# A hybrid decoder step on one core: four weight units split in the value projection and kept in DRAM, key squares in large tiles, norm factors two steps later

## The chip, the cores and the metric

The kernel runs on one core of a Trainium2 chip as one program. The metric is the device time of that program in microseconds; lower is better. The engines of the core are named as in the profile: PE (TensorE, matrix products; PEld is its weight load), DVE (VectorE), ACT (ScalarE), POOL (GpSimd) and SP (SyncE, which here only issues transfers). Sixteen DMA engines move data between DRAM and the on-chip memory (SBUF); PE writes its results into banks of PSUM.

## The reference

Two layers of a decoder trunk in float32, over one prompt of 1024 tokens and eight single tokens with state from before. The first layer mixes tokens by a gated recurrence (RG-LRU), the second by grouped-query attention in a window of 128 with a sink for each head. Behind each mixer stands a squared-ReLU MLP, ahead of each block an RMS norm, and each block is added to the residual. The part that matters here:

```python
def qkv_heads(x, w_qkv, q_g, k_g):
    q, k, v = jnp.split(x @ w_qkv, [Q_DIM, Q_DIM + KV_DIM], axis=-1)
    q = rms_norm(q.reshape(n, t, N_KV, GROUP, HEAD_DIM), q_g)
    k = rms_norm(k.reshape(n, t, N_KV, HEAD_DIM), k_g)
    v = v.reshape(n, t, N_KV, HEAD_DIM)

def swa_prompt(x, w_qkv, q_g, k_g, sinks, w_out, w_buf):
    q, k, v = qkv_heads(x, w_qkv, q_g, k_g)
    ...
    o = sink_attention(qb, with_prev(k), with_prev(v), dist, mask[:, None, None], sinks)
    y = o.reshape(n, t, Q_DIM) @ w_out

def sq_relu_mlp(x, w_up, w_down):
    return jnp.square(jax.nn.relu(x @ w_up)) @ w_down
```

The model width is 1024, the query width 1024 (16 heads of 64), keys and values 256 each, the MLP's inner width 4096.

## The kernel before

**Data.** Activations lie transposed: eight tiles of 128 channels by 1032 tokens (1024 and the 8 single ones), worked on in three chunks of 344 tokens. A weight matrix comes in units of 128 x 1024 elements (512 KB). A float32 value goes to PE as a rounded upper half and the rest, each in PE's own format: three products (upper by upper, lower by upper, upper by lower) replace one. For this each unit is loaded into a "raw" tile, ACT casts the upper half ("wh", L180) and DVE subtracts it from the raw to get the lower ("wl", L181), for units of the attention in two pieces of 128 x 512 each. The list `units` fixes the order of the loads; `ensure(k)` splits all units up to k and has the next two raw tiles fetched; `unit(name, j)` hands a split unit to its product.

**Stages.** 0 to 330 us: the recurrent layer. Then the first MLP to 958 us, whose products (L582) follow a table of steps, `PROG`, built on Strassen's scheme. Then attention to about 1303 us with its output projection, and from about 1318 us the second MLP.

**Attention.** Query tile 0 and key tile 0 are projected first; then the second key tile (`proj_steps`, L912), the values (`v_proj`, L942), and the query tiles 1 to 7 as filler, whose steps stand between the 32 steps g of the scores. At step g the scores (bank "SS", one buffer, L1006) are masked, exponentiated, transposed (bank "T", L1033), copied by ACT (L1035), multiplied by DVE (pt, L1037) and taken to the values on PE (bank "O", one buffer, L1053). The outputs go to DRAM (od) and come back in three chunks (oh, ol; `load_o`, L1179). From g = 22 the filler is the early part of the second output projection ("wo1", L241), in the order 4, 5, 0, 1, 2, 3 of its inputs; inputs 4 and 5 stay on chip, inputs 0 to 3 come back by `load_o`. Its weight units 0 to 3 are split one by one at g = 20, 21, 23 and 24.

**Key norm.** A chunk of keys leaves PSUM by `take_out`: ACT squares it into one small tile (sq, L820) and copies it into another (x, L821). The two key tiles' norms then run one after the other (`k_evac`, `k_norm`): PE adds the squares across channels into bank "N" (one buffer, L827), DVE reads that bank (L828) and so gives it back, then some steps on ACT and DVE make the factor, and the key's halves are sent on by SP and POOL.

**Order.** Each engine runs its rows strictly in the order of the program that a scheduler wrote down from the data and buffer dependences; the score steps are pinned in the order of the code. SP issues transfers in its own order, and the eight semaphores of its queue rotate, so that a transfer also waits for the one eight places ahead to have landed. A tile of a pool (A 33 large, W 12, S 9 small ones, R 2 raw) is handed out again when its last reader is done.

**Norm factors.** In both MLPs the sum of squares of the last chunk is turned into the factors of the norm at step 7 of `PROG` (`factors`, then `swap_small`); the factors are read first at step 12.

Of the kernel before, what the change touches and what calls it, by code (L numbers as in the profile page):

```python
# [10 lines left out]
F32 = mybir.dt.float32  # L11
# [51 lines left out]
def trunk(ctx: ExitStack, tc: tile.TileContext, I, O):  # L63
# [38 lines left out]
    def A(s="a"):  # L102
        return A2(s)[:, 0:T]
# [4 lines left out]
    def S(s="s"):  # L108
        return small["pool"].tile([P, CH], F32, tag="S", name=nm(s))
# [30 lines left out]
    def cs(c):  # L140
        return slice(c * CH, (c + 1) * CH)
# [25 lines left out]
    def fetch(n):  # L167
        while len(raws) < min(n, len(units)):
            name, _, src, _ = units[len(raws)]
            if name[:2] == "dn":  # L170
                raws.append(small["pool"].tile([P, D], F32, tag="Q", name=nm("raw")))
            else:
                raws.append(R("raw"))
            sp.dma_start(raws[-1][:, 0:src.shape[1]], src)
# [9 lines left out]
    units = []  # L184
    loaded = {}

    def add_units(name, src, n, alloc=lambda j: W):
# [23 lines left out]
    def ensure(k):  # L211
        while nloaded[0] <= min(k, len(units) - 1):
            n, j, _, alloc = units[nloaded[0]]
            fetch(nloaded[0] + (NRAW if n[:2] == "dn" else 2))
            if alloc is None:
                loaded[(n, j)] = raws[nloaded[0]]
            else:
                loaded[(n, j)] = split_unit(raws[nloaded[0]], alloc, dve,
                                            2 if nloaded[0] < 4 or n in ("q", "k", "v", "wo1") else 1)
            nloaded[0] += 1  # L220
# [431 lines left out]
    def mlp_products(layer, tok, pw, r, acc, gnext, store):  # L652
# [25 lines left out]
        for n, (kind, q, i) in enumerate(PROG):  # L678
            up = kind == "up"
            w, x = BY[i]  # L680
            if up and n in (1, 3, 5, 7, 9):
                tok.make(("B22", "T3", "T2", "T4", "T1")[n // 2])
            if n == 7:
                factors(rs.pop("late"), DB())
                swap_small(f"u{layer}", 3)
# [116 lines left out]
    def attention(hs):  # L802
# [14 lines left out]

        def take_out(o):
            s, x = S("sq"), S("x")
            act.activation(s, o, AF.Square)  # L820
            act.copy(x, o)  # L821
            return s, x
# [104 lines left out]
        def vblk(b, p):  # L927
            h = b // 4
            o = (b % 4) * 256 + p * P
            return v_tiles[h][:, o:o + P]  # L930

        def v_proj():
            w = [unit("v", 0, 1), unit("v", 1, 1)]

            def mms(o, sl):
                n = 0
                for k in range(M8):
# [3 lines left out]
                    for xt, wt in ((xh, wh), (xh, wl), (xl, wh)):  # L941
                        pe.matmul(o, lhsT=r_(xt[:, sl]), rhs=r_(wt[:, ws]), start=(n == 0), stop=(n == 3 * M8 - 1))  # L942
                        n += 1

            for b2 in range(NB // 2):
                ps = B("S")
                for j in range(2):
# [5 lines left out]
                if b2 == 3:  # L953
                    vo = S("vo")
                    act.activation(vo[:, :256], ps[:, 256:512], AF.Copy, scale=fx["rt"][:, NB - 1:NB])
                    sp.dma_start(O["v"], vo[:, :256])
            ps = B("T")
            mms(ps[:NS, :256], slice(SEQ, T))
# [181 lines left out]
        for rows in ((1, 0, 3, 2), (5, 4), (7, 6)):  # L1140
            for i, c, o in firsts:
# [4 lines left out]
                if rows[-1] == 4 and i:  # L1146
                    tokens(rs["sq"][:, cs(c)], c)
        sk, xk = A("sk"), A("xk")
        for i, c, o in firsts:
            if i:  # L1150
                act.activation(sk[:, cs(c)], o, AF.Square)
                act.copy(xk[:, cs(c)], o)
            else:
                q_evac(0, c, o)

        def keys(c, o):
            sx = take_out(o)
            k_evac(0, c, (sk[:, cs(c)], xk[:, cs(c)]), fx["row"][:, cs(c)])
            if c == 0:
                by_token()  # L1160
            return lambda: k_evac(1, c, sx, fx["row"][:, cs(c)])
# [36 lines left out]

        NG = 4 * NB
        AHEAD, G0 = 2, 22  # L1200
        FILL = {0: 51, 6: 90, 14: 136, G0: 177}
# [37 lines left out]
        for g in range(NG):  # L1239
# [21 lines left out]
            if g == 17:  # L1261
                for t in (4, 5):
                    ohl[t] = (A("oh"), A("ol"))
            if g in (20, 21, 23, 24):
                ensure(index["wo1", (20, 21, 23, 24).index(g)])
            if g == G0 - 1:
# [371 lines left out]
```

## Time and profile before

| | us |
|---|---|
| median of three runs | 1947.93 |
| lowest and highest run | 1946.99 and 1949.74 |
| the profiled execution's own time | 1948.49 |
| its span in the profile | 1946.7 |
| granted TensorE clock | 1.0 |
| busy: DVE, ACT, POOL | 1482.5, 1010.0, 364.4 |

The page cuts the span into 40 equal slices and gives the busy share of each in tenths; this is how the work of the engines lies over the stages:

```
DVE  7996747987777968787753777589877779687884
ACT  6585635443434635555654666465443436455552
POOL 1320000000000322332123667000000003223321
DMA  5111242244445778888744436622443447788877
```

A slice is 48.7 us. The attention lies in slices 20 to 27: there POOL works too, and the DMA engines reach 6 tenths just before the output projection's end. Durations of groups stand behind a bar as the busy time and the mean of one in ns, then the idle time ahead of them with what ended it. In a timeline a row has the start, the duration, the engine and line, and in brackets the wait ahead of it.

### The profile page before, as it was taken

To read this page: it belongs to the slowest core of one execution; us is meant where nothing else is said; L and a number is where in the kernel's file an instruction comes from. 1 tells how busy PE (TensorE), PEld (TensorE's weight loads), DVE (VectorE), ACT (ScalarE), POOL (GpSimd) and SP (SyncE) were. 2 spreads that over 40 slices of the span, in tenths; PEclk is the share of its full clock that TensorE was granted. 3 is DMA by queue.
4 is the path that set the end of the run, shared out by engine and by line. 5 is a ranking of instruction groups with operands and counts; after the bars stand their busy time and mean duration, and the time that the engine had idled before them with its cause. 6 is when DMAs were issued, how large, how long until landed. Compare 5 with 4: busy or idle time off the path is not lost.

```text
span 1946.7 us, 34178 instructions
## 1 busy us (share of the span) xinstructions
PE 1932.7 (99%) x12820; PEld 1797.6 (92%) x12820; DVE 1482.5 (76%) x2713; ACT 1010.0 (52%) x1999; POOL 364.4 (19%) x709
## 2 busy tenths in 40 slices
PE   9999999999999999999999999999999999999999
PEld 9999999999999999999999887999999999999998
DVE  7996747987777968787753777589877779687884
ACT  6585635443434635555654666465443436455552
POOL 1320000000000322332123667000000003223321
PEclk9999999999999999999999999999999999999999
DMA  5111242244445778888744436622443447788877
GB/s 195 35 46 53 77 160 84 99 164 158 141 155 171 264 207 196 213 237 217 203 124 112 111 108 199 209 84 99 163 147 137 162 167 260 216 193 218 235 197 183
DMA packets 114149, 311.34 MB, mean 160 GB/s; under 512 B 17464, under 2 KB 43072, under 8 KB 113984
## 3 DMA queue, kind: packets, MB, share of 16 engines
q0 software_dynamic: 31264, 105.77, 22.5%
q1 hardware_dynamic: 57376, 135.68, 21.0%
q10 hardware_dynamic: 25344, 67.71, 9.7%
q8 instruction: 101, 1.65, 0.4%
q14 instruction: 64, 0.52, 0.1%
HBM read 179.67 MB, written 116.75 MB: 152 GB/s over the span
## 4 chain that ended last, share of the span: by engine, by line
PE 91%; DVE 4%; ACT 3%; DMA 1%; issue 1%; POOL 0%; SPq 0%; DVEq 0%; ACTq 0%
PE bD L582 37%; PE bZ L582 27%; PE bP L241 10%; PE bS L241 6%; PE bT L241 3%; PE bP L912 3%; PE bO L1053 1%; PE bSS L1006 1%; ACT se L1019 1%; PE bS L942 1%; DVE op L432 1%; PE bT L1033 1%; PE bP L1144 0%; DMA raw<-w_in 0%; DVE wl L181 0%
## 5 line engine op out<-in xcount | busy, mean ns | idle before, releaser
L582 PEld LDWEIGHTS bD<-tl,op 128*128 128x128 f32 x3072 | 385.5, 188 | 11.7 <-DVE ho L733 0.6
L582 PE MATMUL bD<-tl,op 128*128 128x260 f32 x3072 | 389.2, 282 | 0.2
L582 PEld LDWEIGHTS bD<-op,op 128*128 128x128 f32 x3072 | 380.4, 188 | 7.8
L582 PE MATMUL bD<-op,op 128*128 128x260 f32 x3072 | 382.9, 282 | 0.0
L595 POOL DMA_DIRECT2D tl<-hsum x224 | 131.5, 662 | 897.8 <-PE bD L582 411.7
L431 ACT CAST op<-ws 128x512 fp32r<-128x512 f32 (+1 forms) x288 | 162.1, 572 | 255.6 <-DVE ws L550 128.2
L582 PE MATMUL bZ<-tl,op 128*128 128x512 f32 x1152 | 288.2, 394 | 0.0
L582 PE MATMUL bZ<-op,op 128*128 128x512 f32 x1152 | 282.1, 394 | 0.0
L582 PEld LDWEIGHTS bZ<-op,op 128*128 128x128 f32 x1152 | 210.5, 188 | 43.8 <-ACT he L718 0.2
L582 PEld LDWEIGHTS bZ<-tl,op 128*128 128x128 f32 x1152 | 207.9, 188 | 40.4 <-DVE tl L439 0.4
L439 DVE TENSOR_TENSOR tl<-tl 128x520 fp32r<-128x520 f32 (+1 forms) x224 | 145.3, 691 | 76.2 <-ACT tl L438 76.2
L431 ACT CAST op<-raw 128x512 fp32r<-128x512 f32 (+1 forms) x216 | 123.5, 573 | 145.8 <-PE bD L582 82.5
L432 DVE TENSOR_TENSOR op<-ws,op 128x512 fp32r<-128x512 f32 (+1 forms) x288 | 176.0, 625 | 8.6 <-ACT op L431 8.4
L432 DVE TENSOR_TENSOR op<-raw,op 128x512 fp32r<-128x512 f32 (+1 forms) x216 | 134.8, 625 | 7.2 <-ACT op L431 6.3
L438 ACT CAST tl<-tl 128x520 fp32r<-128x520 f32 (+1 forms) x224 | 124.9, 626 | 4.6 <-DMA tl<-hsum 1.9
L733 DVE TENSOR_TENSOR ho<-bD,ho 128x520 f32<-128x520 f32 x140 | 97.4, 696 | 37.3 <-PE bD L582 35.3
L181 DVE TENSOR_TENSOR wl<-raw,wh 128x512 fp32r<-128x512 f32 (+1 forms) x72 | 61.0, 868 | 31.4 <-ACT wh L180 14.9
L722 DVE TENSOR_TENSOR ho<-bZ,ho 128x512 f32<-128x512 f32 x72 | 49.5, 688 | 43.7 <-PE bZ L582 43.2
L724 ACT COPY he<-bZ 128x512 f32<-128x512 f32 x68 | 39.9, 587 | 80.5 <-PE bZ L582 66.0
L706 ACT COPY he<-bZ 128x512 f32<-128x512 f32 x72 | 42.0, 583 | 74.7 <-PE bZ L582 73.6
L733 DVE TENSOR_TENSOR he<-bD,he 128x520 f32<-128x520 f32 x70 | 48.8, 696 | 37.5 <-PE bD L582 37.3
L180 ACT CAST wh<-raw 128x512 fp32r<-128x512 f32 (+1 forms) x72 | 53.0, 764 | 43.6 <-PE bT L241 14.2
(372 smaller groups left out, 3653.9 us busy)
## 6 DMA issues: line engine op xcount, KB each, us to landing
tl<-hsum POOLq DMA_DIRECT2D x128, 260.0 KB, 6.4
raw<-w_up SPq DMA_DIRECT2D x64, 512.0 KB, 4.2
tl<-hsum POOLq DMA_DIRECT2D x96, 256.0 KB, 6.5
raw<-w_dn SPq DMA_DIRECT2D x64, 384.0 KB, 6.2
hsum<-ts ACTq DMA_DIRECT2D x32, 520.0 KB, 4.0
hsum<-ho ACTq DMA_DIRECT2D x32, 516.0 KB, 3.6
hsum<-he ACTq DMA_DIRECT2D x32, 516.0 KB, 2.7
spill<-ho POOLq DMA_DIRECT2D x32, 516.0 KB, 6.8
```

The costliest lines, as they stand in the source:

```text
L180: act.copy(r_(hi[:, sl]), raw[:, sl])
L181: eng.tensor_tensor(r_(lo[:, sl]), raw[:, sl], hi[:, sl], ALU.subtract)
L241: pe.matmul(o, lhsT=r_(wt[:, col(k):col(k) + P]), rhs=r_(xt[:, cs(c)]), start=(k == first and a == 0), stop=(k == final and a == 2))
L431: act.copy(r_(hi), x)
L432: dve.tensor_tensor(r_(lo), x, hi, ALU.subtract)
L438: act.copy(r_(hi), lo)
L439: eng.tensor_tensor(r_(lo), lo, hi, ALU.subtract)
L582: pe.matmul(d[:, 512 * b:512 * b + c], lhsT=r_(wt[:, j * P:j * P + P]), rhs=r_(xt[:, c * b:c * b + c]), start=first and j == 0 and a == 0, ...
L595: pool.dma_start(t[:, n:2 * n], src)
L722: dve.tensor_tensor(o0, d, o[:, HP], ALU.add)
L733: last["sum"] = dve.tensor_tensor(t, inner(d), t, ALU.add).ins
L912: pe.matmul(o, lhsT=r_(wt[:, k * P:k * P + P]), rhs=r_(xt[:, cs(c)]), start=(k == 0 and a == 0), stop=(k == M8 - 1 and a == 2))
```

## The change

It has four parts. `split_to_store` is new: in the value projection, for each of the four pairs of blocks, one of the units 0 to 3 of wo1 is loaded into a large tile (pl), cast (ph) and subtracted in place in two pieces, and both halves are stored in DRAM (eight stores of 512 KB). `fetch` leaves those units out, and `ensure` loads the two halves straight into the tiles of the product (eight loads of 512 KB), two units at g = 17 and two at g = 21. The squares and copies of both key tiles are written into two pairs of large tiles (`held`). And `factors` with `swap_small` stands at step 9 of `PROG` instead of step 7, in both MLPs.

```diff
@@ -166,7 +166,10 @@
 
     def fetch(n):
         while len(raws) < min(n, len(units)):
-            name, _, src, _ = units[len(raws)]
+            name, j, src, _ = units[len(raws)]
+            if (name, j) in stored:
+                raws.append(None)
+                continue
             if name[:2] == "dn":
                 raws.append(small["pool"].tile([P, D], F32, tag="Q", name=nm("raw")))
             else:
@@ -183,6 +186,7 @@
 
     units = []
     loaded = {}
+    stored = {}
 
     def add_units(name, src, n, alloc=lambda j: W):
         for j in range(n):
@@ -212,7 +216,11 @@
         while nloaded[0] <= min(k, len(units) - 1):
             n, j, _, alloc = units[nloaded[0]]
             fetch(nloaded[0] + (NRAW if n[:2] == "dn" else 2))
-            if alloc is None:
+            if (n, j) in stored:
+                loaded[(n, j)] = alloc("wh"), alloc("wl")
+                for t, d in zip(loaded[(n, j)], stored[(n, j)]):
+                    sp.dma_start(t[:, 0:D], d)
+            elif alloc is None:
                 loaded[(n, j)] = raws[nloaded[0]]
             else:
                 loaded[(n, j)] = split_unit(raws[nloaded[0]], alloc, dve,
@@ -680,7 +688,7 @@
             w, x = BY[i]
             if up and n in (1, 3, 5, 7, 9):
                 tok.make(("B22", "T3", "T2", "T4", "T1")[n // 2])
-            if n == 7:
+            if n == 9:
                 factors(rs.pop("late"), DB())
                 swap_small(f"u{layer}", 3)
             if (kind, q, i) == ("up", NU, 4):
@@ -815,8 +823,8 @@
         den = [cp.tile([P, 12], F32, name=f"den{i}") for i in range(3)]
         dd = aux[:, 2 * P + 2 * NS:2 * P + 2 * NS + 4]
 
-        def take_out(o):
-            s, x = S("sq"), S("x")
+        def take_out(o, c, sx):
+            s, x = [y[:, cs(c)] for y in sx]
             act.activation(s, o, AF.Square)
             act.copy(x, o)
             return s, x
@@ -929,6 +937,18 @@
             o = (b % 4) * 256 + p * P
             return v_tiles[h][:, o:o + P]
 
+        def split_to_store(n, j):
+            stored[n, j] = [tc.dram_tile([P, D], F32, name=f"{n}{j}{x}") for x in "hl"]
+            lo, hi = A("pl")[:, 0:D], A("ph")[:, 0:D]
+            sp.dma_start(lo, units[index[n, j]][2])
+            yield
+            for x in (slice(0, D // 2), slice(D // 2, D)):
+                act.copy(r_(hi[:, x]), lo[:, x])
+                dve.tensor_tensor(r_(lo[:, x]), lo[:, x], hi[:, x], ALU.subtract)
+            for d, x in zip(stored[n, j], (hi, lo)):
+                sp.dma_start(d, x)
+            yield
+
         def v_proj():
             w = [unit("v", 0, 1), unit("v", 1, 1)]
 
@@ -942,7 +962,11 @@
                         pe.matmul(o, lhsT=r_(xt[:, sl]), rhs=r_(wt[:, ws]), start=(n == 0), stop=(n == 3 * M8 - 1))
                         n += 1
 
+            ready = iter(())
             for b2 in range(NB // 2):
+                next(ready, None)
+                ready = split_to_store("wo1", b2)
+                next(ready)
                 ps = B("S")
                 for j in range(2):
                     b = 2 * b2 + j
@@ -954,6 +978,7 @@
                     vo = S("vo")
                     act.activation(vo[:, :256], ps[:, 256:512], AF.Copy, scale=fx["rt"][:, NB - 1:NB])
                     sp.dma_start(O["v"], vo[:, :256])
+            next(ready, None)
             ps = B("T")
             mms(ps[:NS, :256], slice(SEQ, T))
             vo = S("vo")
@@ -1145,17 +1170,17 @@
                                   start=(k == 1 and a == 0), stop=(k == 6 and a == 2))
                 if rows[-1] == 4 and i:
                     tokens(rs["sq"][:, cs(c)], c)
-        sk, xk = A("sk"), A("xk")
+        held = [(A("sk"), A("xk")) for _ in range(2)]
+        out = []
         for i, c, o in firsts:
             if i:
-                act.activation(sk[:, cs(c)], o, AF.Square)
-                act.copy(xk[:, cs(c)], o)
+                out.append(take_out(o, c, held[0]))
             else:
                 q_evac(0, c, o)
 
         def keys(c, o):
-            sx = take_out(o)
-            k_evac(0, c, (sk[:, cs(c)], xk[:, cs(c)]), fx["row"][:, cs(c)])
+            sx = take_out(o, c, held[1])
+            k_evac(0, c, out[c], fx["row"][:, cs(c)])
             if c == 0:
                 by_token()
             return lambda: k_evac(1, c, sx, fx["row"][:, cs(c)])
@@ -1197,6 +1222,7 @@
         fill = filler()
 
         NG = 4 * NB
+        AT = (17, 17, 21, 21)
         AHEAD, G0 = 2, 22
         FILL = {0: 51, 6: 90, 14: 136, G0: 177}
         EARLY = {G0 + 0.3: 0, NG: 48}
@@ -1261,8 +1287,8 @@
             if g == 17:
                 for t in (4, 5):
                     ohl[t] = (A("oh"), A("ol"))
-            if g in (20, 21, 23, 24):
-                ensure(index["wo1", (20, 21, 23, 24).index(g)])
+            for _ in range(AT.count(g)):
+                ensure(nloaded[0])
             if g == G0 - 1:
                 for t in range(4):
                     load_o(t, cs(0))
```

**What moves: the key-norm sums on PE.** Rows of PE around the sum of the second key tile's second chunk (the bank is bN, its squares sq before and sk in a large tile now; bP is the second key projection's third chunk and bS the value projection). Before, in the value projection:

```order
L942 MATMUL bS1383_10827<-wh1378_10813,hh1290_10267 128x256
L942 MATMUL bS1383_10827<-wl1379_10814,hh1290_10267 128x256
L942 MATMUL bS1383_10827<-wh1378_10813,hl1291_10268 128x256
L827 MATMUL bN1361_10712<-sq1354_10682,con_73 128x344
L942 MATMUL bS1383_10827<-wh1378_10813,hh1287_10251 128x256
L942 MATMUL bS1383_10827<-wl1379_10814,hh1287_10251 128x256
```

Now, in the key projection's third chunk, whose first eight products stand between this sum and the one before it (the sum of the first key tile's chunk, also in bank N):

```order
L920 MATMUL bP1358_10706<-hl1236_9855,wh1329_10555 128x344
L920 MATMUL bP1358_10706<-hh1235_9854,wl1330_10556 128x344
L920 MATMUL bP1358_10706<-hh1277_10150,wh1329_10555 128x344
L920 MATMUL bP1358_10706<-hl1278_10151,wh1329_10555 128x344
L835 MATMUL bN1359_10710<-sk1317_10513,con_73 128x344
L920 MATMUL bP1358_10706<-hh1277_10150,wl1330_10556 128x344
```

The sum stood behind 24 products of the third key chunk and 15 of the values, and now stands behind 8 of the key chunk.

**What moves: ACT at the end of the value projection.** Before (vt and vo are the scaled values and the value output, qc the copy of the first query tile's sums, wh a unit's upper half):

```order
L952 ACTIVATE vt1299_10325<-bS1385_10929,st_330 128x256 x2
L180 CAST wh1391_11068<-raw1380_10819 128x512 x2
L952 ACTIVATE vt1299_10325<-bS1386_10980,st_330 128x256 x2
L955 ACTIVATE vo1387_11031<-bS1386_10980,st_330 128x256
L960 ACTIVATE vo1389_11059<-bT1388_11034,st_330 8x256
L868 COPY qc1395_11085<-bN1394_11084 128x256
L311 ACTIVATE q1399_11112<-qs1397_11109,st_330 128x16
```

Now (ph is the upper half of a w_out unit that goes to DRAM):

```order
L976 ACTIVATE vt1299_10325<-bS1387_10952,st_330 128x256 x2
L183 CAST wh1395_11108<-raw1376_10815 128x512 x2
L976 ACTIVATE vt1299_10325<-bS1390_11014,st_330 128x256 x2
L979 ACTIVATE vo1391_11065<-bS1390_11014,st_330 128x256
L946 CAST ph1386_10950<-pl1385_10949 128x512 x2
L985 ACTIVATE vo1393_11099<-bT1392_11074,st_330 8x256
L946 CAST ph1389_11012<-pl1388_11011 128x512 x2
L876 COPY qc1399_11125<-bN1398_11124 128x256
L319 ACTIVATE q1403_11152<-qs1401_11149,st_330 128x16
```

Four casts of ph, in two rows of two, stand between the value output vo and the copy qc; the last two wait for the load of pl that SP issues behind the value output.

**What moves: DVE and SP ahead of the output projection.** Rows of DVE from the subtraction for wo1's unit 0 to unit 1 before (se is the score tile, lo a query's lower half, st the single tokens' part, den the sums of the exponentials, pt the transposed probabilities):

```order
L181 TENSOR_TENSOR wl1645_12986<-raw1559_12354,wh1644_12985 128x512 x2
L1014 TENSOR_TENSOR se1302_10330<-bSS1646_12991,se1302_10330 128x4x128
L853 TENSOR_TENSOR lo1648_13029<-bP1639_12945,hi1647_13028 128x344
L1015 TENSOR_REDUCE den2_10323<-se1302_10330 128x4
L857 TENSOR_TENSOR st_330<-bP1639_12945,st_330 64x8
L1016 SCALAR_TENSOR_TENSOR den2_10323<-den2_10323,st_330 128x4
L857 TENSOR_TENSOR st_330<-bP1639_12945,st_330 64x8
L1037 TENSOR_TENSOR pt1650_13039<-bT1649_13038,side1300_10327 128x512
L181 TENSOR_TENSOR wl1655_13057<-raw1643_12983,wh1654_13056 128x512 x2
```

Now:

```order
L1038 COPY_PREDICATED bSS1650_13029<-side1300_10327,bSS1650_13029 128x4x128
L1039 TENSOR_TENSOR se1302_10330<-bSS1650_13029,se1302_10330 128x4x128
L1040 TENSOR_REDUCE den2_10323<-se1302_10330 128x4
L861 TENSOR_TENSOR lo1652_13067<-bP1646_12991,hi1651_13066 128x344
L1041 SCALAR_TENSOR_TENSOR den2_10323<-den2_10323,st_330 128x4
L865 TENSOR_TENSOR st_330<-bP1646_12991,st_330 64x8 x2
L1062 TENSOR_TENSOR pt1654_13077<-bT1653_13076,side1300_10327 128x512
L884 TENSOR_TENSOR qs1677_13147<-bN1655_13085,st_330 128x16
```

The four subtractions in two rows are gone, and the other rows follow one another in the same order but for lo. SP's rows of the first chunk of the attention output's way back before (q and its parts hi and lo are the last query tile's):

```order
L1179 DMA oh1656_13062<-od0h_10331 128x344
L859 DMA q01625_12827<-hi1637_12937 64x344
L859 DMA q11626_12828<-hi1637_12937 64x344
L1179 DMA ol1657_13063<-od0l_10332 128x344
L1179 DMA oh1658_13066<-od1h_10333 128x344
L860 DMA q01625_12827<-lo1638_12938 64x344
L860 DMA q11626_12828<-lo1638_12938 64x344
L1179 DMA ol1659_13067<-od1l_10334 128x344
L1179 DMA oh1660_13070<-od2h_10335 128x344
L1179 DMA ol1661_13071<-od2l_10336 128x344
L1179 DMA oh1662_13074<-od3h_10337 128x344
L1179 DMA ol1663_13075<-od3l_10338 128x344
```

Now (the halves of wo1's units 2 and 3 are wo12h to wo13l):

```order
L222 DMA wl1658_13093<-wo12l_10948 128x1024
L222 DMA wh1660_13098<-wo13h_11009 128x1024
L222 DMA wl1661_13099<-wo13l_11010 128x1024
L1204 DMA oh1662_13102<-od0h_10331 128x344
L1204 DMA ol1663_13103<-od0l_10332 128x344
L1204 DMA oh1664_13106<-od1h_10333 128x344
L1204 DMA ol1665_13107<-od1l_10334 128x344
L867 DMA q01632_12873<-hi1651_13066 64x344
L867 DMA q11633_12874<-hi1651_13066 64x344
L868 DMA q01632_12873<-lo1652_13067 64x344
L868 DMA q11633_12874<-lo1652_13067 64x344
L1204 DMA oh1666_13110<-od2h_10335 128x344
```

Three loads of halves stand ahead of od0, and the third chunk's query pieces stand ahead of od2 and od3, which before stood behind the second chunk's.

## The prediction

> **What bounds the kernel now.** I read the page first: which engine is busy, and what the chain that ended last runs through.
>
> ```profile
> PE 1932.7 (99%) x12820; PEld 1797.6 (92%) x12820; DVE 1482.5 (76%) x2713; ACT 1010.0 (52%) x1999; POOL 364.4 (19%) x709
> ...
> PE 91%; DVE 4%; ACT 3%; DMA 1%; issue 1%; POOL 0%; SPq 0%; DVEq 0%; ACTq 0%
> ```
>
> TensorE is busy 99% of 1946.7 us and holds 91% of the chain. The change adds and removes no matrix product, so it can only change the time in which PE waits. The list of PE's waits says how much there is:
>
> ```profile
> PE bO L1053 <- DVE pt L1037: 2.4, 2, 1.5
> PE bN L827 <- ACT sq L820: 1.6, 1, 1.6
> PE bSS L1006 <- DVE se L1014: 1.3, 3, 0.7
> PE bN L1293 <- POOL warm L1291: 1.1, 1, 1.1
> PE bSS L1006 <- DVE den L1021: 0.8, 1, 0.8
> PE bD L278 <- DVE slo L276: 0.5, 1, 0.5
> PE bP L241 <- ACT ri L1414: 0.4, 1, 0.4
> PE bN L871 <- ACT qc L868: 0.3, 1, 0.3
> PE bT L1033 <- POOL se L1023: 0.2, 1, 0.2
> ```
>
> Columns: who waits for whom, microseconds in total, times, the longest. The sum is 8.6 us, under half a per cent of the span. The warm-up (1.1) and the 0.4 of L241 lie outside the change. So **some 7 us is all that can be won**, and I go through the four places where the change touches a row of this list.
>
> **Key squares (L820, L827, L828).** Rows of the timeline around the third chunk of the second key projection:
>
> ```profile
> 999.05 0.62 ACT L180 CAST wh<-raw 128x512 fp32r<-128x512 f32 x1 [1.39 <-DMA raw<-w_qkv]
> ...
> 1000.27 0.74 PE L827 MATMUL bN<-sk,con 128*128 128x344 f32 x2
> ...
> 1002.12 0.32 PE L912 MATMUL bP<-hh,wl 128*128 128x344 f32 x1
> ...
> 1002.92 0.57 DVE L828 SCALAR_TENSOR_TENSOR sk<-ms,st,bN 128x344 f32<-128x344 f32 x1
> ...
> 1008.18 0.85 PE L827 MATMUL bN<-sq,con 128*128 128x344 f32 x2 [1.62 <-ACT sq L820]
> ```
>
> Before, the fourth key-norm sum waited 1.62 us at 1008.18 for a square that ACT took late, because its small tile was still held. In the change the square lies in a tile of its own and is taken early, and the order puts that sum after eight L912 products behind the third sum. PE reaches this place at 1002.12 (the ninth row's start). All sums share one PSUM bank, "N", and it is given back when DVE has done L828 for the third sum: 1002.92 + 0.57 = 1003.49. DVE isn't earlier there, as what stands ahead of it is the same and hangs on the weight that landed at 999.05. So PE now waits 1003.49 - 1002.12 = 1.4 in place of 1.6: **-0.2 us**. Ends: -1.6 (the bank is free in time, the wait goes) and +0.3 (sums five and six, also pulled forward, each a little late; the nearest row is the 0.3 of L871).
>
> **Value projection.** Four units of w_out are loaded, cast, subtracted and stored as two halves. That is 4 x 2 casts and 4 x 2 subtractions, whose price is that of the same operations in the stretch they come from:
>
> ```profile
> L180 ACT CAST wh<-raw 128x512 fp32r<-128x512 f32 x8 | 4.5, 618 | 2.3 <-DMA raw<-w_out 2.3
> ...
> L181 DVE TENSOR_TENSOR wl<-raw,wh 128x512 fp32r<-128x512 f32 x8 | 5.4, 701 | 0.0
> ...
> 1025.00:1030.00 5.00, 5.00 (x45) 5.00 (x44) 2.94 (x6) 2.25 (x5) 2.26 (x5) 1.00 0.59 155
> 1030.00:1035.00 5.00, 5.00 (x44) 4.31 (x43) 0.00 (x0) 1.67 (x4) 0.00 (x0) 1.00 0.63 197
> ```
>
> 4.5 us on ACT and 5.4 on DVE go into a stretch in which (windows: seconds and counts of PE, PEld, DVE, ACT, POOL, then clock, DMA share, GB/s) ACT is busy 2.25 or 1.67 of 5 us and DVE 2.94 or 0. Over some 25 us they are hidden; without that cover they would cost PE nothing directly, but late value copies. The exception is the last unit, since its load goes out only after the value output o_v, and its two casts stand ahead of the query sum's copy (L868) on ACT:
>
> ```profile
> 1032.95 0.34 SPq L956 DMA_DIRECT2D o_v<-vo  x1
> ...
> 1036.53 0.38 ACT L868 COPY qc<-bN 128x256 f32<-128x256 f32 x1 [1.55 <-PE bN L866]
> ...
> 1038.41 0.38 PE L871 MATMUL bN<-con,qc 128*128 128x128 f32 x2
> ...
> DMA to landing us min/median/max: 4.3/5.2/6.2
> ```
>
> The last row is the landing of the 512 KB loads of w_qkv (L174) in 995 to 1045. The load is issued at about 1032.95 + 0.3 = 1033.2. I take the shortest landing, 4.3, because the traffic is thinnest there: few other transfers are left after 1033: 1037.5. Two casts in 1.14 us (0.52 and 0.62), then the copy of 0.38: 1039.0, against 1038.4 where PE wants it. **+0.6 us**; with 6.2 it is +2.5; with a landing under 3.7 nothing, so the ends are 0 and +2.5. What queues behind the waiting casts on ACT is that copy and the three small steps of the query norm, and PE alone waits for it.
>
> The Trainium skill, "DMA: Bandwidth & Descriptors", section "Anatomy of one DMA — SWDGE (gpsimd) path", gives about 2.0 us plus bytes over 436 GB/s; worked out for 512 KB that is an estimate of 3.2 us, by which this term would be 0 and the sum 0.6 lower. Our row's shortest is 4.3, so I go by the row. The same section says that the receipt of a write is slowest where the target is DRAM, which speaks against storing halves.
>
> The page has stores and loads of that size:
>
> ```profile
> raw<-w_up SPq DMA_DIRECT2D x64, 512.0 KB, 4.2
> ...
> hsum<-ho ACTq DMA_DIRECT2D x32, 516.0 KB, 3.6
> ```
>
> The stores landed in 3.6 us, the loads in 4.2: no dearer, so by these rows the receipt costs nothing that a load does not, and the halves are wanted only from 1157. At 155 to 197 GB/s before, eight stores and four loads of 0.5 MB (6 MB over some 35 us, 170 GB/s more) stay under the 372 GB/s that the stretch 1185 to 1190 moved (its row stands with the third rival).
>
> **Second output projection (1160 to 1200).** Here the casts and subtractions of w_out stood between the attention's own steps:
>
> ```profile
> 1175.66 0.60 DVE wl L181
> ...
> 1178.49 0.70 DVE pt L1037
> ...
> 1179.24 0.65 PE L1053 MATMUL bO<-pt,se 128*64 128x256 f32 x4 [1.51 <-DVE pt L1037]
> ...
> 1188.19 0.52 DVE L383 TENSOR_TENSOR x<-bP,x 128x344 f32<-128x344 f32 x1 [1.76 <-DMA x<-spill]
> ...
> 1190.03 0.65 PE L1053 MATMUL bO<-pt,se 128*64 128x256 f32 x4 [0.88 <-DVE pt L1037]
> 1190.79 1.12 ACT L180 CAST wh<-raw 128x512 fp32r<-128x512 f32 x2
> ...
> 1191.52 0.36 PE L1006 MATMUL bSS<-kh,q 128*128 128x256 f32 x1 [0.84 <-DVE den L1021]
> ```
>
> The first two rows are of the chain, which steps through DVE's queue there without a break. (a) The wait of 1.51: two subtractions, 0.60 each, leave the queue ahead of pt: 1.51 - 1.20 = 0.3 remains. (b) 0.88: one subtraction goes (0.60), and the wait for x now stands behind pt, but the mask copy, one more step of 0.6, moves ahead of it: I take half, 0.45 remains. (c) 0.84: two casts of 1.12 leave ACT ahead of the exponentials that this den needs: 0.2 remains. The two small rows (0.3 of se, 0.2 of POOL) stay. So 3.7 us of waits become 1.45.
>
> What is late next is the attention output, read back in pieces (od, oh, ol) on SP. Before, and after by the order, SP's rows there:
>
> ```profile
> 1171.29 2.06 SPq L1179 DMA_DIRECT2D oh<-od2h  x1
> ...
> 1174.39 0.38 SPq L1179 DMA_DIRECT2D ol<-od3l  x1
> ...
> 1177.24 1.11 SPq L859 DMA_DIRECT2D q<-hi  x2
> ...
> 1183.80 0.32 PE L241 MATMUL bP<-oh,wh 128*128 128x344 f32 x1
> ...
> oh<-od3h SPq DMA_DIRECT2D x2, 172.0 KB, 3.0
> ```
>
> od2 and od3 of the first chunk were issued from 1171.29 to 1174.39. In the changed order three half loads, od0 and od1 and four query pieces stand ahead of them. The query pieces began at 1177.24; their cast no longer stands behind two of w_out (1.1 us), so they begin at about 1176.1, take 4 x 0.55 = 2.2, and the four pieces of od2 and od3 go from 1178.3 to 1179.5 (0.4 each). With 3.0 to land the last is there at 1182.5. PE took od3's first product at 1183.80 and wants it 1.2 earlier when (a) is won, at 1182.6, and od2 half a microsecond before: I put 0.25 of wait. Sum of this place: -3.7 + 1.45 + 0.25 = **-2.0 us**. Ends: -3.5 (nearly all waits go) and +3.4 (landing as in the third rival).
>
> **Factors at step 9 instead of 7.** The row of L278 (0.5) is a product whose operand DVE makes at the start of the last MLP; the two steps moved behind it free DVE there, and the first MLP has no such row: **-0.5 us**, ends -0.5 and 0. The factors are first used at step 12, so three steps of PE work still cover them; without that cover they cost their own two operations.
>
> **The sum:** -0.2 + 0.6 - 2.0 - 0.5 = -2.1 us, on the profiled execution's 1948.49 us (span 1946.7, some 1.8 around it that the change leaves alone): 1946.4. That execution lies 0.56 above the median of the runs, 1947.93, so against the median it is **1945.8 us**.
>
> **The rivals.** *More goes (A):* the key bank is free in time (-1.6), the last casts aren't late (0), (a) to (c) leave little (-2.5), -0.5: together -4.6, 1943.3 us. For it: ACT and DVE are half idle in the value projection; against: the bank's release hangs on a DMA's landing. *Nothing is won (B):* a wait goes and the next one takes its place at each PE stop: 0 for the keys, +0.6, 0 for the attention, -0.5: 1948.0 us. For it: the key wait does just this by my own sum, and the attention's steps form a ring (scores, exponentials, products) in which the next link may be as late. It is also the case in which the change does not do what it says. *Slower (C):* loads that land as under load. In 1185 to 1190 the DMA engines are full (0.99), and pieces of the same kind take longer:
>
> ```profile
> 1185.00:1190.00 5.00, 4.15 (x32) 3.20 (x30) 3.24 (x8) 2.24 (x8) 2.84 (x8) 1.00 0.99 372
> ...
> ol<-od1l SPq DMA_DIRECT2D x1, 168.0 KB, 5.9
> ```
>
> If od2 and od3 take the 5.9 us of a later piece instead of 3.0, they land from 1184.2 to 1185.4 against a want of 1182.1 to 1182.6: a wait of 2.8, and 0.6 more in the next chunk's pieces, which SP issues only behind these, 3.4 in all, while (a) to (c) only move behind it; the last w_out load at 6.2 adds 2.5: -0.2 + 2.5 + 3.4 - 0.5 = +5.2, 1953.1 us. It decides from where od's landing passes some 3 us; the row of 3.0, some 4 us earlier in the kernel, speaks against it.
>
> **How the numbers follow.** A measurement of this kernel tells about 0.2% (3.9 us) from no change: faster is below 1944.0, slower above 1951.8. Forecast 0.46, its own range 1944.0 to 1947.2; A 0.24; B 0.19; C 0.11. A lies mostly below 1944.0, and a tail of the forecast too: faster 0.28. C's larger part is above 1951.8: slower 0.09. Same 0.63. The range takes in A down to the best ends (-1.6, 0, -3.5, -0.5: 1942.3) with 0.8 for the spread of the runs, 1941.5, and B with the lighter part of C to 1950.5.
>
> **What would show it.** Keys: PE's wait for sq (1.6) gone, and one of about 1.4 for DVE's L828, now some 6 us earlier, in its place; if neither is there, A. Values: a wait of PE for qc of 0.6. Attention: rows for pt and den at 1 us together instead of 3.2; if rows for oh or ol from DRAM stand there, C. Factors: the slo row gone from the list. Wrong would be the whole if PE's busy time itself changed, or if a wait came up in the first layers, where only the factors move.

## The result, and the profile after

| | before | after |
|---|---|---|
| median of six runs each | 1948.53 | 1956.26 |
| lowest and highest | 1946.99 and 1949.74 | 1955.59 and 1961.62 |
| ratio of the runs, 95% interval | | 1.0042 [1.0031, 1.0053] |
| mean granted clock | 1.0 in the profiled one | 0.998 in five runs, 0.995 in the profiled one |

The kernel became 7.7 us slower, outside the range given. The first view is the list of PE's waits in the changed kernel (lines are some 8 to 25 higher than before: L868 is L876 now, L871 is L879, L827 is L835, L1053 is L1078):

```profile
PE bN L879 <- ACT qc L876: 5.2, 2, 5.0
PE bSS L1031 <- DVE se L1039: 1.6, 2, 0.9
PE bN L835 <- ACT hi L846: 1.5, 1, 1.5
PE bO L1078 <- ACT pt L1060: 1.4, 2, 0.7
...
PE bP L249 <- DMA ol<-od3l: 0.8, 1, 0.8
PE bP L1169 <- DVE he L739: 0.6, 1, 0.6
PE bZ L590 <- ACT he L726: 0.5, 1, 0.5
PE bT L1058 <- DVE pt L1062: 0.4, 1, 0.4
...
PE bO L1078 <- DVE pt L1062: 0.3, 1, 0.3
```

One row is new in size: 5.0 us of waiting for the copy of the query sums, the wait that the prediction had at 0.6. The rows of pt (1.5 and 0.9 before), of den (0.8) and of slo (0.5) are smaller or gone, and rows for a load from DRAM and twice for he have come. But the waits grew by less than the time did. The second view is the windows of the changed kernel around that wait (seconds and counts of PE, PEld, DVE, ACT, POOL, then the granted clock, the DMA share, GB/s):

```profile
1036.00:1040.00 4.00, 3.81 (x28) 2.90 (x26) 0.00 (x0) 0.00 (x0) 0.00 (x0) 1.00 1.01 306
1040.00:1044.00 4.00, 0.00 (x0) 0.00 (x0) 1.31 (x3) 2.18 (x5) 0.00 (x0) 1.00 0.99 397
1044.00:1048.00 4.00, 3.21 (x12) 3.21 (x13) 1.97 (x4) 2.67 (x9) 0.00 (x0) 0.50 0.93 370
1048.00:1052.00 4.00, 4.00 (x19) 4.00 (x18) 1.69 (x7) 0.41 (x2) 2.15 (x6) 0.65 0.46 150
1052.00:1056.00 4.00, 4.00 (x28) 4.00 (x27) 0.52 (x1) 0.80 (x2) 1.75 (x5) 1.00 0.55 138
```

PE stands for all of 1040 to 1044, and when it goes on it has **half its clock**: 0.50, then 0.65 over the next four microseconds. That costs 3.2 x 0.50 + 4.0 x 0.35 = 3.0 us of busy time. 5.0 + 3.0 = 8.0 is the whole of the loss of 7.7 and a little more. (The Trainium skill, "TensorE: Matmul & The Clock Gate", section "Part 1: The HAM clock gate (the "warmup" mystery)", has this: PE falls to half its clock after an idle window of about 3.4 us and needs a busy one to come back. The trace agrees on the half, and the dip (the stretch at half clock) lasts 6.8 us, the first window and 2.8 us of the second, twice that window. It does not agree on how long a pause is needed, as runs 3 and 5 below show, and there the measurement decides.)

Where the time went is seen when the same product of PE, by its number in the order of starts (the first is 0), is looked up in both traces:

```
product  start before  start after  later by
 2280       363.38        364.17       0.79   first MLP
 6300       968.84        970.56       1.72   attention begins
 6600      1018.00       1019.30       1.30   in the value projection
 6890      1057.18       1065.94       8.76   behind the wait and the half clock
 7670      1165.33       1174.66       9.33   ahead of the output projection
 7850      1193.97       1201.14       7.17   in its first part
 7910      1203.01       1211.76       8.75   some 10 us on
 8280      1256.61       1269.83      13.22   a second dip, in the profiled execution alone
12819      (end of the last MLP)     12.92
```

The first row differs by as much from one execution to the next. So the start of attention lost 0.9, the key part won 0.4, the value projection lost 7.5, the query tiles behind it 0.6, and the output projection won 2.2 and gave 1.6 back within 9 us. How the last two loads came so late is in rows of SP, ACT and PE in the timeline of the changed kernel, and behind them in its chain of waits, which has the load itself (start, length):

```profile
1016.55 0.51 SPq L943 DMA_DIRECT2D pl<-w_out  x1
1020.78 0.33 SPq L949 DMA_DIRECT2D wo10h<-ph  x1
...
1030.63 4.16 SPq L907 DMA_DIRECT2D kh<-hi  x4
1034.83 0.59 SPq L949 DMA_DIRECT2D wo11l<-pl  x1
1035.51 0.40 SPq L943 DMA_DIRECT2D pl<-w_out  x1
1036.01 0.72 SPq L177 DMA_DIRECT2D raw<-w_qkv  x1
1036.82 0.45 SPq L980 DMA_DIRECT2D o_v<-vo  x1
1037.32 0.42 SPq L943 DMA_DIRECT2D pl<-w_out  x1
...
1040.44 1.14 ACT L946 CAST ph<-pl 128x512 fp32r<-128x512 f32 x2 [6.24 <-DMA pl<-w_out]
...
1043.33 1.14 ACT L946 CAST ph<-pl 128x512 fp32r<-128x512 f32 x2 [1.39 <-DMA pl<-w_out]
...
1044.79 0.69 PE L879 MATMUL bN<-con,qc 128*128 128x128 f32 x2 [4.98 <-ACT qc L876]
```

The chain of waits:

```profile
1037.32 5.91 DMA pl<-w_out
```

The fourth unit's load went out at 1037.32, four microseconds later than I had worked out, behind a store, the third unit's load, a load of w_qkv and the value output, and took 5.91 instead of 4.3. ACT runs its rows in order, so the copy that PE needed stood behind casts that waited for these loads (6.24 us for the third unit's, 1.39 for the fourth's).

Two rows more tell how SP fell behind: the first of its list of waits from 1005 to 1046 (7.4 us in two waits, the longest 3.8), and four key pieces as it issued them in the kernel before.

```profile
SPq L949 <- ACT ph L946: 7.4, 2, 3.8
...
1026.73 2.38 SPq L899 DMA_DIRECT2D kh<-hi  x4
```

The first of the two waits, from 1017.06 to 1020.78, is SP before the first store, until ACT had cast the first unit; from 1025.96 to 1037.74 it issued with hardly a pause, and four key pieces took it 4.16 us instead of 2.38. So the value output, which ACT had ready at 1034.20, went out at 1036.82.

### The profile page after: what moved, and what is told of

The parts are those of the page before. It is cut to its first block, busy times and chain, and to the rows that moved or that the text cites. A ratio compares the mean times of both kernels' runs of the same rounds, so it can differ in the third digit from the quotient of the medians.

```text
span 1959.8 us, 34180 instructions
## 1 busy us (share of the span) xinstructions
PE 1940.4 (99%) x12820; PEld 1804.6 (92%) x12820; DVE 1482.2 (76%) x2713; ACT 1010.6 (52%) x1999; POOL 360.8 (18%) x709
## 4 chain that ended last, share of the span: by engine, by line
PE 90%; DVE 4%; ACT 2%; DMA 2%; issue 1%; SPq 0%; POOL 0%; DVEq 0%; ACTq 0%; POOLq 0%
PE bD L590 36%; PE bZ L590 27%; PE bP L249 10%; PE bS L249 6%; PE bP L920 3%; PE bT L249 3%; PE bS L962 1%; PE bO L1078 1%; PE bSS L1031 1%; ACT se L1044 1%; DVE op L440 1%; PE bT L1058 1%; DMA raw<-w_in 0%; DMA he<-spill 0%; PE bP L1169 0%
## 5 line engine op out<-in xcount | busy, mean ns | idle before, releaser
L184 DVE TENSOR_TENSOR wl<-raw,wh 128x512 fp32r<-128x512 f32 (+1 forms) x64 | 55.6, 891 | 32.1 <-ACT wh L183 15.5
L1044 ACT ACTIVATE se<-se,den,st 128x129 f32<-128x129 f32 x128 | 61.8, 487 | 23.1 <-DVE den L1041 20.3
```

What stands on the lines that cost most here:

```text
L184: eng.tensor_tensor(r_(lo[:, sl]), raw[:, sl], hi[:, sl], ALU.subtract)
L1044: act.activation(se[:, x, :], se[:, x, :], AF.Exp, scale=f[:, v, 0, u:u + 1], bias=dn[:, 4 + x:5 + x], accum_out=dn[:, 8 + x:9 + x])
```

## The experiments

Times are medians beside runs of the kernel before on the same chip (their medians are 1947.61 to 1947.93 us); ratios have their 95% interval.

**1. The change without the four units.** Keys and factors alone; `v_proj` and `ensure` as before.

```diff
-                next(ready, None)
-                ready = split_to_store("wo1", b2)
-                next(ready)
...
-            for _ in range(AT.count(g)):
-                ensure(nloaded[0])
+            if g in (20, 21, 23, 24):
+                ensure(index["wo1", (20, 21, 23, 24).index(g)])
```

> The change without its part on the four weight units: key squares in large tiles and factors at step 9 only; wo1 is split as before. Theory S (the loss is PE's wait of 5.0 us for the query sums' copy behind the late casts, and the half clock after it): none of it is here, so no wait for that copy over 0.5 us, mean clock 1.0, and 1947.0 to 1949.0 us. Theory K (the key tiles or the factors bring part of the loss): over 1950.5 us.

Measured: 1947.52 us, 0.9998 [0.9989, 1.0007]. The wait for the copy is 0.3 again. Theory K falls; the loss is in the part on the units. The mean clock is 1.0 in ten of eleven runs; the profiled one, at 0.999, has a dip elsewhere, which stands with the last section.

**2. Only the four units**, keys and factors as before.

> Only the part on the four weight units; keys and factors as before. The order has the copy of the query sums behind the casts of the third unit, but ahead of those of the fourth. Theory S: the wait of PE for the copy is about 2 us, as the third unit's load lands at about 1040.5; the clock stays at 1.0 or dips once; 1949.0 to 1951.5 us. Theory D (the twelve added transfers of 512 KB cost time wherever they stand): about 1956 us.

Measured: 1952.45 us, 1.0022 [1.0013, 1.0030], between the two answers and in neither. The place was a miss as well: the copy waits 0.3, but another row leads the list of PE's waits:

```profile
PE bN L835 <- ACT sq L828: 3.9, 2, 2.2
```

And the windows there:

```profile
1016.00:1020.00 4.00, 2.00 (x17) 1.79 (x16) 1.90 (x5) 1.80 (x4) 0.00 (x0) 1.00 0.99 271
1020.00:1024.00 4.00, 3.78 (x19) 3.58 (x20) 2.67 (x5) 3.26 (x8) 2.06 (x4) 0.69 0.92 271
```

With small key tiles it is the square of a key chunk that ACT takes late, at 1019.72, behind the first unit's casts, which waited 2.24 us for their load; and the clock dips after it too (0.69, the window behind the wait). In the change, with its large tiles, no row for sq stands in the list. The mechanism is one: ACT in order, casts that wait for a load, and whatever stands behind them.

**3. The fourth unit's casts behind the copy.** The transfers stay as they are.

```diff
-            act.copy(q, st[:, 0:2 * P])
-            yield from range(4)
+            last["qc"] = act.copy(q, st[:, 0:2 * P]).ins
+            yield
+            if pend:
+                with tc.issue_after(last["qc"]):
+                    next(pend.pop(), None)
+            yield from range(3)
...
-            next(ready, None)
+            pend.append(ready)
```

> The whole change, with the fourth unit's two casts set behind the copy of the query sums on ACT; the same transfers are made. Theory S: PE waits for the copy about 2 us instead of 5.0, 1949.0 to 1951.5 us. Theory D: the transfers are the same, about 1956 us.

Measured: 1953.17 us (1950.40 to 1955.47), 1.0026 [1.0017, 1.0035]. The wait was 2.0 us as expected, but the time is 1.7 above what S said: after a wait of only 2.0 us the clock dipped as well, 0.79 in each of two windows of 4 us.

**4. Both last units' casts behind the copy.** As 3, with the third unit's casts moved too.

> The whole change, with the third and the fourth unit's casts behind the copy of the query sums. Theory S: no wait for the copy over 0.5 us, no dip of the clock, 1946.5 to 1949.0 us, unless the query tile's own casts, which now stand behind the late ones, hold PE for up to 1.5 us. Theory D: about 1956 us.

Measured: 1948.51 us, 1.0004 [0.9995, 1.0013]. All twelve transfers of the value projection are still made, and the loss is gone within the noise: from product 6600 to 6890 this kernel takes 0.45 us more than before, where the change took 7.5 more. Theory S holds, and theory D, the price of the transfers wherever they stand, falls. What the change was to win has not come either; run 10 takes that up.

**5 to 7. The wait by itself.** The kernel before, with the copy repeated, so that PE waits with no transfer added.

```diff
+            for _ in range(19 if t == 0 else 0):
+                act.copy(q, st[:, 0:2 * P])
             act.copy(q, st[:, 0:2 * P])
```

> The kernel before, with the copy of the first query tile's sums done ten times over on ACT, so that PE's next product behind it waits; no transfer is added. By 0.33 us for a copy and 1.5 us of slack PE waits about 1.5 us. Theory G (a long wait of PE by itself makes the clock drop): before has waits of 1.5 and 1.6 us at a clock of 1.0, so the clock stays, and the time is 1949.0 to 1950.0 us. Theory H (the dip belongs to the added transfers, not to the wait): the same here.

> The same with the copy done fifteen times: PE waits about 3.1 us. Theory G: as after the wait of 2.0 us in the run with the fourth unit's casts moved, the clock dips in most executions, at a price of 1 to 3 us: 1951.5 to 1954.5 us. Theory H: clock 1.0, the wait alone, 1950.5 to 1951.3 us.

> The same with the copy done twenty times: PE waits about 4.8 us, as in the changed kernel, but with no transfer added. Theory G: half clock for some 6 us in every execution, as in the changed kernel: 4.8 + 3.0, 1955.0 to 1956.5 us. Theory H: clock 1.0, 1952.2 to 1953.0 us.

| copies | PE's wait, us | median, us | ratio | mean clock of the runs |
|---|---|---|---|---|
| 10 | 2.0 | 1951.38 | 1.0019 [1.0009, 1.0028] | 0.996 to 1.0, below 1.0 in 6 of 10 |
| 15 | 4.0 | 1953.78 | 1.0030 [1.0019, 1.0041] | 0.998 to 0.999 in 7 of 7 |
| 20 | 6.1 | 1955.54 | 1.0040 [1.0026, 1.0055] | 0.997 to 0.998 in 5 of 5 |

The waits came out longer than I had worked out (a copy took 0.40 us from one start to the next, not 0.33). In run 5 neither answer is met, as both had the clock at 1.0 behind a wait of 1.5 us. But with no transfer added the clock falls in all three kernels, so theory H falls and G's cause holds: a wait alone halves the clock. That run 7's time lies in G's range is partly luck: 4.8 + 3.0 was worked out, and 6.1 + 1.5 came. The windows of the longest wait show when:

```profile
1040.00:1042.00 2.00, 0.00 (x0) 0.00 (x0) 0.00 (x0) 1.84 (x6) 0.00 (x0) 0.91 0.00 0
1042.00:1044.00 2.00, 0.00 (x0) 0.00 (x0) 0.00 (x0) 1.84 (x6) 0.00 (x0) 0.50 0.00 0
...
1046.00:1048.00 2.00, 2.00 (x9) 2.00 (x9) 0.66 (x4) 1.46 (x6) 0.00 (x0) 0.50 0.00 0
1048.00:1050.00 2.00, 2.00 (x13) 2.00 (x12) 1.88 (x5) 0.99 (x2) 1.54 (x2) 0.89 0.32 73
```

0.91 in the first of these means full clock to 1041.64, and 0.89 in the last that it is back from 1048.44: 6.8 us at half. The windows of the shortest wait:

```profile
1040.00:1042.00 2.00, 0.60 (x4) 0.60 (x5) 0.05 (x1) 1.26 (x4) 0.00 (x0) 0.93 0.00 0
1042.00:1044.00 2.00, 2.00 (x9) 2.00 (x8) 0.29 (x2) 1.57 (x6) 0.00 (x0) 0.50 0.00 0
1044.00:1046.00 2.00, 2.00 (x11) 2.00 (x10) 1.97 (x7) 0.77 (x2) 0.16 (x1) 0.72 0.00 0
```

Here it goes from 1041.72 to 1045.12: 3.4 us, half as long. What a dip costs is half of the time that PE works in it: 1.5 us after the wait of 6.1, most of whose dip fell into the wait itself, and 1.7 us after the wait of 2.0. From product 6600 to 6890 the three profiled executions take 3.8, 6.4 and 7.3 us more than before.

**8. The factors alone at step 9.**

> The kernel before with the factors at step 9 alone. My term: the wait of 0.5 us for slo at the start of the last MLP goes and nothing takes its place, 0.5 us less. Rival: the waits for he that stand in the traces with the change, 0.4 to 0.5 in the last MLP and 0.6 to 1.0 at the start of attention, come from this move, and it gives back what it wins: 1947.5 to 1948.5 us, with those two rows in the list of waits.

Measured: 1949.01 us, 1.0009 [1.0000, 1.0018], above the rival's range too. My term has the wrong sign, though only just clear of the noise. The rival's two rows are there, and slo's is gone:

```profile
PE bP L1144 <- DVE he L731: 0.6, 1, 0.6
...
PE bZ L582 <- ACT he L718: 0.4, 1, 0.4
```

Such a pair of waits stands in the traces of all seven kernels with the move (the change, 1, 3, 4, 8, 9 and 12), and in none of 2, 5, 6, 7, 10 and 11, which have the factors at step 7. What the first of them costs can be read without the noise of whole runs: from product 2280 to 6300, the first MLP, the seven traces with step 7 (the kernel before among them) all take 605.5 us, and the seven with step 9 take 606.1 to 606.7.

**9. The stores on POOL.** Same bytes; SP issues only the loads.

```diff
             for d, x in zip(stored[n, j], (hi, lo)):
-                sp.dma_start(d, x)
+                pool.dma_start(d, x)
```

> The whole change, with the eight stores of the halves issued by POOL instead of SP; the same bytes move, and in the order the fourth unit's load stands ahead of SP's last key pieces. Theory Q (SP's queue, in which stores that wait for a subtraction or for a place among eight hold up the loads behind them, makes the last load late): that load goes out at least 3 us earlier than 1037.3, PE waits for the query sums' copy 1.5 us or less, 1948.0 to 1951.0 us. Theory L (the added traffic makes every landing late): the wait stays at 4 to 5 us, about 1956 us.

Measured: 1954.0 us (1951.32 to 1960.13), 1.0037 [1.0025, 1.0048], from only six runs. Each theory has half of it. The view of the loads' line has the four issues (shortest, median, longest in ns, first and last start) and, below, the landing:

```profile
L943 SPq DMA_DIRECT2D pl<-w_out x4: 591/772/1073, 1011.9 to 1030.6; - x4
...
DMA to landing us min/median/max: 7.7/7.7/7.7
```

The last load goes out at 1030.6 instead of 1037.3, so SP's queue did hold it up (the order also has it ahead of the last key pieces and of the value output here); but the one load whose landing is known, the third unit's, took 7.7 us, so the landing counts too. PE waited 1.8 us for the copy, and the clock was below 1.0 in four of six runs. In the profiled execution (1952.29 us) the clock doesn't dip, and the value projection takes 1.6 us more than before; the rest of this kernel's loss lies elsewhere and was not followed up.

**10. The halves of units 2 and 3 loaded behind the pieces od.** Run 4 showed the waits of the output projection being won and then given back. The row that gave them back is a wait of DVE for the residual x, and PE's wait behind it:

```profile
1187.97 1.96 SPq L423 DMA_DIRECT2D x<-spill  x4
...
1194.09 0.52 DVE L391 TENSOR_TENSOR x<-bP,x 128x344 f32<-128x344 f32 x1 [2.12 <-DMA x<-spill]
...
1197.30 0.35 PE L1040 MATMUL bSS<-kh,q 128*128 128x256 f32 x1 [1.63 <-DVE se L1048]
```

The first x went out at 1181.92 before and at 1187.97 here, as SP had three half loads and then query pieces ahead of the second half of od, and x behind those. The edits to run 4's kernel:

```diff
-            if n == 9:
+            if n == 7:
                 factors(rs.pop("late"), DB())
...
-        AT = (17, 17, 21, 21)
+        AT = (17, 17, 23, 24)
```

> The kernel with the third and fourth unit's casts behind the copy, with two more edits: the halves of units 2 and 3 are loaded at g = 23 and 24 instead of 21, so that SP's order has the pieces od and the first x ahead of them as before; and the factors stand at step 7 again. Theory X (the waits won at the output projection were given back because od and x went out late on SP): the waits for ol from DRAM and the wait of 1.6 us for se at 1197 go, some 1.5 us less than that kernel, and the factors' wait for he at the start of attention goes too: 1945.5 to 1947.5 us. Rival (the ring of attention steps gives the gain back anyway): 1947.5 to 1949.0 us.

Measured: **1945.76 us** (1945.42 to 1946.22), 0.9989 [0.9981, 0.9998], the only kernel here whose interval lies below 1, if only by a little. Between 1160 and 1210 its list of waits has these left, 1.9 us against 3.7 before:

```profile
PE bSS L1040 <- DVE se L1048: 0.8, 1, 0.8
PE bO L1087 <- ACT pt L1069: 0.7, 1, 0.7
PE bT L1067 <- DVE pt L1071: 0.4, 1, 0.4
```

Theory X holds: from product 7670 to 7850 this kernel wins 3.5 us, and at 7880 it has 3.1 of them. That is against the profiled execution before; runs 5 to 8, whose code is the same there, took 0.7 to 0.9 less in this stretch than that execution did, so 2.5 to 2.8 is nearer.

**11. Stores on POOL, late half loads, factors at step 7**, with the casts where the scheduler puts them.

> Stores on POOL, halves of units 2 and 3 at g = 23 and 24, factors at step 7; casts where the scheduler puts them. By theories Q and X together: no wait for the copy over 0.5 us, no wait for ol, 1945.0 to 1947.5 us. If only one of the two holds: 1948 to 1951 us.

Measured: 1949.84 us, 1.0011 [1.0002, 1.0019]: only X holds. PE waits 3.2 us for the copy, and the clock is below 1.0 in eight of eleven runs. Here the order on ACT is the cure, and not another queue for the stores.

**12. Run 10's kernel with the factors at step 9.**

> The kernel that was 1945.76 us, but with the factors at step 9 as in the change. It parts the two edits of that kernel: by the run of the factors alone the move costs 0.5 to 1.3 us, so 1946.3 to 1947.0 us with the waits for he at the start of attention and in the last MLP back in the list. Rival: the factors' place makes no difference beside the place of the loads, 1945.5 to 1946.0 us.

Measured: 1947.01 us, 0.9996 [0.9987, 1.0005]; just at the upper end of the first answer, with the two rows for he back (0.3 and 0.4). That is 1.25 us more than run 10, or 0.9 when each is taken beside its own runs of the kernel before, which were on different chips; in run 8 the move cost 1.4. Each difference is of the size of its interval, but both have the same sign, and the first MLP shows the cost by itself (run 8).

## Why the prediction was wrong

- **"It can only change the time in which PE waits"** was the wrong frame. PE's busy time went from 1932.7 to 1940.4 us with the same 12820 products: 3.0 us of it because a wait of some length halves the clock behind it, the rest by a second dip that only the profiled execution had. Runs 5 to 7 show the first by itself. The prediction named this as what would upset it, but gave it no chance and no price.
- **Value projection, the step that failed:** "The load is issued at about 1032.95 + 0.3 = 1033.2. I take the shortest landing, 4.3". It went out at 1037.32 and landed after 5.91. That is 4.1 of issue and 1.6 of landing. With the 0.6 of the sum, and less the 1.4 by which PE itself came later to its product (1039.81 instead of 1038.41), it makes 4.9, and 5.0 was measured. I had priced the added transfers on the value output's time of before, as if SP had the same queue ahead of it. In fact SP had stood 3.7 us before the first store, and issued with hardly a pause after 1025.96, so that the value output itself went out at 1036.82 instead of 1032.95. Why an issue took longer there isn't shown; the list of SP's waits from 1005 to 1046 names ACT, DVE and PE, and no transfer, so no wait for a place among the eight in flight shows there. And the traffic that I called thin was full: the DMA share is 0.80, 1.01 and 0.99 in the windows from 1032 to 1044 of the changed trace, and 0.29 and 0.00 in those from 1032 to 1040 before. The estimate of 3.2 us for such a load, which the prediction set aside, was further off still; its section is on transfers that POOL issues, as its title says, and this load is SP's. The mechanism, casts ahead of the copy on ACT, was the right one; runs 3 and 4 show it by moving the casts alone.
- **Output projection:** the sum of (a) to (c) came out, but not by its parts. 1.45 us of wait was to remain, and up to product 7850 rows for pt of 0.4, 0.7 and 0.3 do, 1.5 in all; only the 0.3 stands at one of the three places, that of (a). (b) and (c) went wholly, and the other two rows are new, so that the sum fits is luck. For od 0.25 was worked out and 0.8 came. Up to there 2.2 us were won against 2.0 worked out (1.2 to 1.5 against runs 5 to 8, whose code is that of before there). "What is late next" was wrong: I looked at od and took x for harmless. x stood behind od on SP, and 1.6 was given back. Run 10, which moves the half loads behind them, keeps nearly all of the gain.
- **Keys:** right. The wait of 1.6 became one of 1.46 some microseconds earlier (-0.2 worked out, 0.4 won). The list names ACT's hi as the releaser, not DVE's step on the bank (L828, now L836); by the timeline they end at 1005.43 and 1005.40, and PE goes on at 1005.54, so the bank was given back as late as the prediction had it.
- **Factors:** -0.5 was wrong in sign. The wait for slo went, but in the last MLP one of 0.4 to 0.5 for he took its place, and the first MLP, which the sum had at nothing because it had no such row, got a new one: 0.6 to 1.2 us more in all seven kernels with the move. The medians say 1.4 (run 8) and 0.9 (run 12). Why a move at step 9 makes he late at the end of the first MLP, some six hundred microseconds on, was not followed up.
- **The rivals:** C had half of the cause, loads that land as under load, but put the larger half at od, where it was worth 0.8. Its price of 5.2 lacked the queue and the clock.

## What to carry to other kernels

Work put into the idle time of an engine that runs in order is free only if its inputs are there: a cast that waits for a load holds up every row behind it. When transfers are added to a queue, work out the issue time of the first needed one again, transfer by transfer, with the longest landing of the trace. And a wait of PE must be priced with the clock behind it: in this kernel a wait of 2.0 us cost 3.8 in the median of run 5, and one of 5.0 some 8.0 by the windows of the change.

## What the runs showed of the hardware that I had not expected

A wait of 2.0 us is enough for the dip, though not in each execution: of the ten runs of experiment 5, four lie from 1948.55 to 1949.92 at a mean clock of 1.0, the wait alone, and six from 1950.89 to 1955.57 at 0.999 and less. The waits of 1.5 and 1.6 us in the kernel before stand at 1.0, or 0.999 in 4 of its 23 runs beside these. (A mean of 0.999 is not a sure sign of a dip in the work: the profiled execution before has half clock in its last 1.5 us too, when PE is done.) The dip came in steps of 3.4 us: 3.4 after the waits of 2.0 to 3.2 (runs 2, 3, 5 and 11), 6.8 after those of 4.0 to 6.1.

Still shorter waits may be enough. In run 1's profiled execution the clock halves at 1192.2 for 3.4 us, behind waits of 0.9 and 0.8 that stand there in the kernel before as well, in whose profiled execution the clock stays. If it isn't a dip without a cause in PE's waits, like the one below, these were enough:

```profile
1190.00:1192.00 2.00, 1.04 (x7) 0.62 (x8) 1.90 (x5) 2.00 (x8) 0.56 (x2) 1.00 0.83 205
1192.00:1194.00 2.00, 2.00 (x11) 1.94 (x10) 2.00 (x6) 0.70 (x4) 2.00 (x5) 0.54 0.95 385
1194.00:1196.00 2.00, 2.00 (x11) 2.00 (x10) 1.34 (x3) 2.00 (x10) 1.73 (x5) 0.61 1.00 323
```

So no length of wait that is safe can be given from these runs.

The profiled execution of the change had a second dip with no wait of PE near it, and PE busy throughout:

```profile
1256.00:1260.00 4.00, 4.00 (x30) 4.00 (x29) 1.98 (x7) 1.18 (x3) 0.00 (x0) 0.88 0.20 73
1260.00:1264.00 4.00, 4.00 (x17) 4.00 (x17) 0.77 (x2) 1.72 (x4) 0.00 (x0) 0.50 0.25 88
1264.00:1268.00 4.00, 4.00 (x16) 4.00 (x17) 0.85 (x3) 0.96 (x2) 0.00 (x0) 0.50 0.12 44
1268.00:1272.00 4.00, 4.00 (x23) 3.98 (x23) 1.82 (x6) 1.97 (x5) 0.00 (x0) 0.84 0.13 44
```

It lasted 10.2 us, three of the steps, and cost 0.48 + 2.0 + 2.0 + 0.64 = 5.1 us, nearly all of the 5.4 by which that run (1961.62) lies above the median (1956.26). One run of the kernel before (1953.30 us) and two of run 8 (1953.11 and 1953.44), all at a mean clock of 0.997, may have had one like it. Its cause stays open.
